# A two-layer hybrid mixer: the last layer's merge and output with tokens on partitions, and work that needs no stream at the border of the layers

## The chip, the cores and the metric

One core of a Trainium2 chip runs the whole kernel. The metric is device time in microseconds from launch to end. The kernel before was timed three times: 1225.44, 1225.52 and 1230.26, a median of 1225.52. Besides these there is one profiled execution, from which every duration below is read.

The engines are TensorE (PE; its weight loads are shown apart as PEld), VectorE (DVE), ScalarE (ACT), GpSimd (POOL) and SyncE (SP, which here issues the DMAs).

## What is computed

Two layers of a mixer with D = 1024 over 256 latent tokens and 256 context tokens. In each layer four branches read one normalised input h. Every branch is gated, projected to D, and summed under a sigmoid gate of its own; one output product, an RMS norm and a gate add the sum to the stream. The second layer computes no context output.

```python
def merge_branches(ys, h, w, w_branch_l, w_out_l):
    merged = None
    for r in range(N_BRANCH):
        term = jax.nn.sigmoid(in_proj(h, w, 'gate_%d' % r)) * (ys[r] @ w_branch_l[r])
        merged = term if merged is None else merged + term
    return merged @ w_out_l
...
    for l in range(DEPTH):
        sh_x, sc_x, gt_x = jnp.split(silu_c @ w_ada[l] + b_ada[l], 3, axis=-1)
        hx = rmsnorm(x, g_pre[l]) * (1.0 + sc_x[:, None]) + sh_x[:, None]
        ya, ya_c = na_branch(hx, hc, w, na_rpb[l], cos, sin, rows, with_ctx)
        yb = fourier_branch(hx, w, fnet_w[l])
        yc = gmlp_branch(hx, w, gmlp_norm_g[l], gmlp_ws[l], gmlp_bs[l])
        yd, yd_c = hgrn2_branch(hx, hc, w, lower_bounds[l], hgrn_norm_g[l], with_ctx)
        out_x = merge_branches((ya, yb, yc, yd), hx, w, w_branch[l], w_out[l])
        ...
        x = x + gt_x[:, None] * rmsnorm(out_x, g_post[l])
    return x
```

All is float32. The recurrence (hgrn2) is a chain of chunks, which the kernel works out in seven levels for each stream.

## The kernel before

**Layout.** Nearly everything lies with channels on partitions and tokens in the free dimension: h is kept as `hhi` and `hlo`, a high part and a remainder, [128, 8, 512], where columns 0 to 255 are the latent tokens (stream 0) and 256 to 511 the context (stream 1). Layer 0 works on both, layer 1 on the latent tokens; names carry the layer first (`w1a_g0`, `h10` is layer 1, stream 0).

**Products.** A weight tile is 128x1024 float32, 512 KB, loaded on SP's queue and split into a high part by ACT and a remainder by DVE. A product is then three matmuls for each block of 128 channels: high times low, low times high, high times high. `proj` does eight such blocks (24 matmuls) for 128 output channels, with the weight as the stationary operand and the tokens as the moving one: 512 columns in layer 0, 256 in layer 1. Products whose output lies with tokens on partitions (a_v, c_v, d_i) are already turned round: the tokens are stationary and 512 weight columns move.

**Merge and output.** `merge(r, ...)` does a branch r in eight groups of 128 output channels: a gate product g (24 matmuls), its sigmoid, the branch product g..b (12 matmuls), then on DVE the multiplication and the addition to `mg`. The last branch splits the sum into `mh` and `ml`. `finish(s)` takes these through the output product o (8 times 24 matmuls); for each block ACT squares o (`osq`), DVE sums the squares (`oacc`) and writes `O`, o times the gate G. `residual` then sums over partitions with small matmuls (`r10oss`; the name is layer, stream, o), takes the inverse root in small DVE steps (`r10ov` to `r10o_y`), spreads it over the partitions by a matmul (`r10oR`), multiplies, adds to the residual stream `xr` and sends it out. For layer 0 it goes on to the norm, scale and shift of layer 1 (`r00x..`, `r01x..`), which write hhi and hlo (`scale_shift`).

**Order.** The program is written as a list of tasks, generators that yield between blocks of matmuls. Each engine runs its instructions in the order in which they are issued. Chains that shouldn't hold PE up (recurrence, residual, attention) are spawned as generators of their own; the class `Order` resumes one as soon as a model of the engines' clocks says that its inputs are ready, between two blocks of the main list, or at a `wait(name)`. It also issues the weight loads and splits, at most three raw tiles and four split ones in flight. PSUM has a ring of three tiles for large products (`ps_big`), one of three for small ones (`ps_sm`) and one of one.

**Start.** `start()` goes through the eight channel blocks j. The adaLN row products `ada` run two steps ahead; in step j a small transposition `adaT` of that row gives scale and shift (`scA`, `shB`, on DVE), `scale_shift` makes x into hhi (ACT) and hlo (DVE) of block j, and `more(j)` lets the first five projections (`firstw0d_f_fwd`, ..) take up the blocks below j, so that these products grow block by block.

Of the kernel before, what the change touches and what calls it, by code (L numbers as in the profile page):

```python
# [19 lines left out]
D = 1024  # L20
# [297 lines left out]
def block(ctx: ExitStack, tc: tile.TileContext, a: dict, out: bass.AP):  # L318
# [32 lines left out]
    def big(shape, name, dt=F32):  # L351
        return slot.tile(shape, dt, name=name, tag="slot")
# [148 lines left out]

    def residual(s, x, O, acc, name, last):

        over4 = lambda R: V(R, 0, [[0, 4], [1, 256]])
        R = yield from rms_rows(sum_rows(acc, name + "o"), 2, name + "o")
        if last:
            Rs = t2k.tile([128, 256], F32, name="Rs", tag="t1k", bufs=3)
            act.activation(Rs, R, AF.Copy)
            for eng, js in ((gps, range(6, 8)), (dve, range(0, 2)), (dve, range(2, 4)), (dve, range(4, 6))):
                n, q, c = len(js), js[0] // 4, slice(js[0] % 4, js[0] % 4 + len(js))  # L510
                eng.tensor_tensor(out=O[q][:, c, :], in0=O[q][:, c, :], in1=V(Rs if eng is gps else R, 0, [[0, n], [1, 256]]),
                                  op=ALU.mult)
                eng.tensor_tensor(out=x[q][:, c, :], in0=x[q][:, c, :], in1=O[q][:, c, :], op=ALU.add)
                sync.dma_start(out[:, js[0]:js[0] + n, :], x[q][:, c, :])
            return
        for q in range(2):
            dve.tensor_tensor(out=O[q], in0=O[q], in1=over4(R), op=ALU.mult)
            dve.tensor_tensor(out=x[q], in0=x[q], in1=O[q], op=ALU.add)
            act.activation(O[q], x[q], AF.Square)
        dve.tensor_tensor(out=O[0], in0=O[0], in1=O[1], op=ALU.add)  # L520
        for n in (2, 1):
            dve.tensor_tensor(out=O[0][:, 0:n, :], in0=O[0][:, 0:n, :], in1=O[0][:, n:2 * n, :], op=ALU.add)
        yield
        R = yield from rms_rows(sum_rows(O[0][:, 0, :], name + "x"), 2, name + "x")
        for q in range(2):
            y = O[q]
            dve.tensor_tensor(out=y, in0=x[q], in1=over4(R), op=ALU.mult)
            for jj in range(4):
                scale_shift(4 * q + jj, s, y[:, jj, :])
# [23 lines left out]
    def start(first, rest):  # L553
# [42 lines left out]
        for j in range(NK):  # L596
            dve.tensor_tensor(out=xT[j // 2][:, j % 2, :], in0=xT[j // 2][:, j % 2, :], in1=R, op=ALU.mult)
            if 1 <= j <= len(first):
                key, _ = first[j - 1]
                w = od.take(key)  # L600
                ps = places[j - 1]("first" + key)
                gens.append([proj(ps, w, slice(0, 512)), 0, ps])
            if j + AHEAD < NK:
                rows.append(ada(j + AHEAD))
            more(j)
            tps = ps_hg(f"adaT{j}")[:, 0, :]
            for i in range(2):
                mm(tps[:, 2 * i:2 * i + 2], lhsT=rows[j][:, i * 128:i * 128 + 128], rhs=sel, start=True, stop=True)
            dve.tensor_scalar(out=shB[:, :, j], in0=tps[:, 0:2], scalar1=bada[:, 0, j:j + 1], scalar2=None, op0=ALU.add)
            dve.tensor_scalar(out=scA[:, :, j], in0=tps[:, 2:4], scalar1=bada1[:, j:j + 1], scalar2=gpre[:, 0, j:j + 1],  # L610
                              op0=ALU.add, op1=ALU.mult)
            for s in range(2):
                scale_shift(j, s, xT[j // 2][:, j % 2, s * 256:s * 256 + 256])
        rest()
        for (gen, _, ps), (_, done) in zip(gens, first):
# [33 lines left out]
    def layer(l, stream, first):  # L649
# [450 lines left out]
        def silu_held(ps, name):  # L1100
# [3 lines left out]
            return sh  # L1104

        def fourier_tasks():
            y2 = new_y('B')
            ab = []

            def f():  # L1110
                ab.append(big([128, 4, 256], f"f{l}AB"))
                od.spawn(f"B{l}.w", fourier_weights(ab[0]))
                yield
            task(f)
            for q in range(2):
# [84 lines left out]

        mg2 = bigs(8, nQ, f"mg{l}")
        mh, ml = bigs(8, nQ, f"mh{l}", F32R, "FK" if L0 else None), bigs(8, nQ, f"ml{l}", F32R)
        G = sml.tile([128, 2, 8], F32, name=f"gg{l}", tag="gg", bufs=2)

        def merge(r, y2, need, fill=(), turn=1, ms=range(8), cols=allc):
# [3 lines left out]
            for m in ms:  # L1209
# [35 lines left out]
                task(f)  # L1245

        def finish(s):

            keys = [unit(f"wo{l}{s}{j}", a["wout"][l, j]) for j in range(8)]

            def f():
                x = stream[s]
                if L0:
                    x = [big([128, 4, 256], f"xr{s}{q}") for q in range(2)]
                    for q in range(2):
                        sync.dma_start(x[q], a["xT"][:, 4 * q:4 * q + 4, s, :])
                O = [big([128, 4, 256], f"O{l}{s}{q}") for q in range(2)]
# [19 lines left out]
                stream[s] = x  # L1277
                od.spawn(f"h{l + 1}.{s}", residual(s, x, O, acc, f"r{l}{s}", not L0))
            task(f)
# [18 lines left out]
        if L0:  # L1298
# [15 lines left out]
            merge(2, yC, None, fill[16:])  # L1314
        else:
            wait("h1.0")
            yA, attend = attention_gates()
            yB = fourier_tasks()
# [3 lines left out]
            then(lambda: I_open.__setitem__(0, False))  # L1322
            merge(1, yB, (f"B{l}",), turn=0)
            attend()
            wait(f"D{l}.0")
            hgrn_proj(1)
            merge(0, yA, (f"A{l}",))
            yC = gmlp_tasks()
            merge(2, yC, None)
# [5 lines left out]
        then(gates)  # L1335
        if L0:
            merge(3, yD, None, turn=3, ms=range(LATEM))
            merge(3, yD, None, turn=3, ms=range(LATEM, 8), cols=slice(0, 256))
            finish(0)
            merge(3, yD, None, turn=3, ms=range(LATEM, 8), cols=slice(256, 512))  # L1340
            finish(1)
        else:
            merge(3, yD, None, turn=3)
            finish(0)
        return tasks
# [74 lines left out]
def _layout(p):  # L1420
# [17 lines left out]
    cols = np.concatenate([np.arange(512) + 512 * NAMES.index(n) for n in TGROUPS])  # L1438
    o["wtk"] = c(win[:, :, cols].reshape(2, 4, 2, 128, 3, 512).transpose(0, 4, 1, 3, 2, 5))
    o["wbr"] = c(g["w_branch"].reshape(2, 4, 4, 128, 4, 2, 128).transpose(0, 1, 4, 3, 5, 2, 6).reshape(2, 4, 4, 128, 8, 128))  # L1440
    o["wout"] = c(g["w_out"].reshape(2, 8, 128, 8, 128).transpose(0, 3, 2, 1, 4))
# [32 lines left out]
```

## Time and profile before

| | |
|---|---|
| median of three runs | 1225.52 us |
| the profiled execution's own time | 1227.05 us |
| its span | 1225.2 us |
| granted TensorE clock, mean | 0.994 |
| DMA traffic | 163.35 MB, mean 133 GB/s |
| weight tiles of the gates (wg) | 66 loads of 512 KB, 3.4 us each to landing |
| largest groups of the chain that ended last | PE g 22%, PE a_v 4%, PE ak 4%, PE o 3% |

The page gives busy time, share and number of instructions of each engine for the whole span; PE's busy time is of matmuls that overlap, so a row of one matmul shows a duration longer than the distance to the next. A row of the timeline is start, duration, engine, line, operation, output<-inputs, tile shapes and count; in square brackets stands how long the engine had been idle before it, and whose result ended the wait. A row of the chain of waits is start, duration, engine, tile and count. The windows give the same busy times for a stretch of the span. Every operation goes through a helper, so the lines are nearly all L131 (matmul), L141 (transpose) and L157 (the other engines), and the tile names tell them apart.

### The profile page before, as it was taken

The numbers are of one execution on the slowest core, as the hardware profiler recorded it, in microseconds if no ns is written. First come the engines' busy times: TensorE is split into PE (matmuls) and PEld (weight loads), VectorE is DVE, ScalarE is ACT, GpSimd is POOL, SyncE is SP. The second block draws the span as 40 slices with busy tenths as digits, with TensorE's granted clock in tenths as the row PEclk, the third lists the DMA queues.
The fourth block names the chain that finished last, engine by engine and source line by source line (L and its number), as shares of the span: only waits on it lengthen the run. The fifth ranks groups of instructions, "written<-read, shape, count | busy, mean of one in ns | idle before, by whom it ended". The sixth has DMA issues, their size and how long they took to land.

```text
span 1225.2 us, 21723 instructions
## 1 busy us (share of the span) xinstructions
PE 1182.2 (96%) x9028; PEld 1006.8 (82%) x9028; DVE 782.7 (64%) x1412; ACT 507.9 (41%) x789; POOL 4.8 (0%) x10
## 2 busy tenths in 40 slices
PE   4999999999999999999999999999999999999995
PEld 2677887777788888888888899988898779989995
DVE  5458346765854469746863578968553877866565
ACT  4553324464333222233223346554343555444451
POOL 0000000000000000000000000000000000000000
PEclk9999999999999999999999999999999999999998
DMA  9621222222214245633673374533253324455551
GB/s 364 218 67 65 87 70 90 81 72 86 71 55 144 92 133 193 195 119 115 196 237 105 101 246 153 170 106 122 87 155 121 106 85 129 148 166 170 173 189 52
DMA packets 52034, 163.35 MB, mean 133 GB/s; under 512 B 6752, under 2 KB 13536, under 8 KB 51936
## 3 DMA queue, kind: packets, MB, share of 16 engines
q1 hardware_dynamic: 51936, 161.96, 40.2%
q8 instruction: 71, 1.16, 0.4%
q14 instruction: 27, 0.22, 0.1%
HBM read 160.89 MB, written 1.05 MB: 132 GB/s over the span
## 4 chain that ended last, share of the span: by engine, by line
PE 89%; DVE 6%; ACT 2%; issue 1%; DMA 1%; SPq 0%; ACTq 0%; DVEq 0%
PE g L131 22%; PE a_v L131 4%; PE ak L131 4%; PE o L131 3%; PE zd_f_fwd L131 3%; PE zd_f_bwd L131 3%; PE bx L131 3%; PE aq L131 3%; PE c_v L131 3%; PE d_i L131 3%; PE bg L131 2%; PE dg L131 2%; PE ag L131 2%; PE q L131 2%; PE ao L131 2%
## 5 line engine op out<-in xcount | busy, mean ns | idle before, releaser
L157 ACT ACTIVATE mh<-mg 128x256 fp32r<-128x256 f32 (+1 forms) x18 | 8.7, 488 | 22.3 <-DVE mg L157 22.3
L157 DVE TENSOR_SCALAR F<-F,om,lb 128x512 f32<-128x512 f32 x8 | 4.4, 548 | 20.6 <-ACT F L157 20.6
L157 ACT ACTIVATE osq<-o 128x256 f32<-128x256 f32 x21 | 8.0, 382 | 21.9 <-PE o L131 21.7
L157 DVE TENSOR_TENSOR oacc<-oacc,osq 128x256 f32<-128x256 f32 x21 | 8.9, 423 | 12.6 <-ACT osq L157 12.6
L157 ACT ACTIVATE xT<-xT,shB,scA 128x256 f32<-128x256 f32 x16 | 8.7, 594 | 16.5 <-DVE scA L157 16.5
L157 ACT ACTIVATE QK<-ak 128x512 f32<-128x512 f32 x8 | 4.8, 598 | 25.5 <-PE ak L131 25.5
L157 DVE TENSOR_SCALAR F<-F 128x512 f32<-128x512 f32 x16 | 6.8, 425 | 12.0 <-ACT F L157 12.0
L157 ACT ACT_TABLE_LOAD x11 | 14.1, 1283 | 0.9 <-PEq L1464 0.7
L157 DVE TENSOR_TENSOR ml<-mg,mh 128x256 fp32r<-128x256 f32 (+1 forms) x18 | 9.2, 513 | 7.3 <-ACT mh L157 7.3
L157 DVE TENSOR_SCALAR O<-o,gg 128x256 f32<-128x256 f32 x24 | 11.5, 479 | 2.3 <-ACT oacc L157 2.3
L157 ACT ACTIVATE yhA<-ya 128x512 fp32r<-128x512 f32 (+1 forms) x8 | 4.2, 526 | 20.0 <-DVE ya L157 20.0
L131 PE MATMUL x0ss<-ones,xacc 128*32 128x1 f32 x32 | 0.6, 194 | 12.2 <-DVE xacc L157 12.2
L157 DVE TENSOR_TENSOR Q<-Q,F 128x1024 f32<-128x1024 f32 (+1 forms) x12 | 11.4, 953 | 0.8 <-PE h01d L131 0.4
L157 DVE TENSOR_TENSOR ya<-ao,sa 128x512 f32<-128x512 f32 (+1 forms) x8 | 4.5, 556 | 11.4 <-PE ao L131 11.4
L131 PE MATMUL ada<-wa,cs 128*32 128x256 f32 x128 | 11.6, 465 | 0.0
L131 PEld LDWEIGHTS h00l<-Q,h00ki 64*64 64x64 f32 x448 | 7.6, 135 | 4.5 <-issue 4.1
L157 DVE TENSOR_SCALAR shB<-adaT,c_bada 128x2 f32<-128x2 f32 x8 | 1.8, 222 | 14.6 <-PE adaT L131 14.6
L157 ACT ACTIVATE h01ki<-K 128x1024 f32<-128x1024 f32 x7 | 8.1, 1153 | 7.2 <-DVE K L157 7.2
L157 ACT ACTIVATE h00ki<-K 128x1024 f32<-128x1024 f32 x7 | 8.1, 1162 | 5.9 <-DVE K L157 5.9
L131 PEld LDWEIGHTS x0ss<-ones,xacc 128*32 128x32 f32 x32 | 0.6, 153 | 12.2 <-issue 12.2
L131 PE MATMUL h00l<-Q,h00ki 64*64 64x64 f32 x448 | 8.6, 226 | 1.9 <-DVE Q L157 1.9
L157 ACT ACTIVATE O<-O,shB,scA 128x256 f32<-128x256 f32 x16 | 8.7, 594 | 3.5 <-DVE O L157 3.5
(3335 smaller groups left out, 4599.2 us busy)
## 6 DMA issues: line engine op xcount, KB each, us to landing
wg<-in_win SPq DMA_DIRECT2D x66, 512.0 KB, 3.4
bg<-in_wbr SPq DMA_DIRECT2D x33, 512.0 KB, 3.4
v<-in_wadaT SPq DMA_DIRECT2D x32, 512.0 KB, 3.5
wo<-in_wout SPq DMA_DIRECT2D x24, 512.0 KB, 3.8
wa<-in_wada SPq DMA_DIRECT2D x16, 512.0 KB, 6.8
biast<-in_bias SPq DMA_DIRECT2D x32, 128.0 KB, 2.4
xT<-in_xT SPq DMA_DIRECT2D x4, 512.0 KB, 5.1
w0d_f_fwd<-in_win SPq DMA_DIRECT2D x4, 512.0 KB, 4.7
```

What stands on the lines that cost most here:

```text
L131: self.nc.tensor.matmul(out, lhsT=lhsT, rhs=rhs, **kw)
L157: f(*a, **k)
```

## The change

It has three parts.

**Merge and output of layer 1.** `merge_tokens` takes the place of `merge`, and `finish_tokens` that of `finish`. The tokens are the stationary operand now (128 of them, `tt` 0 and 1) and 512 weight columns move (u 0 and 1); the weights come in new layouts `in_wgt`, `in_wbt` and `in_wot`, again in tiles of 512 KB, each with two blocks of 128 channels by 512 columns. The sum lies in `mT`, tokens on partitions; `turned(u)` transposes it on PE and splits it into mh and ml, spawned as M.0 and M.1 after each half of the last branch. The output product also has tokens on partitions. There the squares are summed by ACT's accumulation (`oss`), `Gr` is the gate spread over the partitions, and the inverse root is one number for each partition, used by one fused multiply and add into `xt`, the residual stream with tokens on partitions. The result is written as (2, 128, 1024).

**The border of the layers.** `fourier_begin` (the tables f10ab, f11ab of the Fourier branch), `gates` and `gate_rows` (Gr) are issued ahead of layer 1's wait for h1.0, and `residual_rows` (xt) behind it.

**The start.** In step j the first projections' turn (`od.take`, `more(j)`) comes behind adaT and scale_shift of that step; before it stood ahead of them.

```diff
-    def residual(s, x, O, acc, name, last):
+    def residual(s, x, O, acc, name):
...
-        if last:
-            Rs = t2k.tile([128, 256], F32, name="Rs", tag="t1k", bufs=3)
-            act.activation(Rs, R, AF.Copy)
...
         for j in range(NK):
             dve.tensor_tensor(out=xT[j // 2][:, j % 2, :], in0=xT[j // 2][:, j % 2, :], in1=R, op=ALU.mult)
-            if 1 <= j <= len(first):
...
-            more(j)
             tps = ps_hg(f"adaT{j}")[:, 0, :]
...
             for s in range(2):
                 scale_shift(j, s, xT[j // 2][:, j % 2, s * 256:s * 256 + 256])
+            if 1 <= j <= len(first):
...
+            more(j)
...
+        def token_product(pss, key, q, last, stat, name):
+
+            hi, lo = od.take(key)
+            for tt in range(2):
+                if q == 0:
+                    pss.append(ps_big(f"{name}{tt}"))
+                c = slice(tt * 128, tt * 128 + 128)
+                for k in range(2 * q, 2 * q + 2):
+                    s = slice(k % 2 * 512, k % 2 * 512 + 512)
+                    mm(pss[tt], lhsT=stat[1](k)[:, c], rhs=hi[:, s], start=k == 0, stop=False)
+                    mm(pss[tt], lhsT=stat[0](k)[:, c], rhs=lo[:, s], start=False, stop=False)
+                    mm(pss[tt], lhsT=stat[0](k)[:, c], rhs=hi[:, s], start=False, stop=k == 2 * last + 1)
...
+        def turned(u):
+
+            for j in (4 * u, 4 * u + 2):
+                ps = ps_sm(f"mt{j}")
+                for k in range(2):
+                    for tt in range(2):
+                        transpose(ps[:, k * 256 + tt * 128:k * 256 + tt * 128 + 128],
+                                  mT(tt)[:, (j + k) * 128:(j + k) * 128 + 128], eye)
+                split(V(mh(j), 0, [[1, 512]]), V(ml(j), 0, [[1, 512]]), ps)
+            yield
+
+        def across(ps_of, src_of, dst, rhs):
+
+            for u in range(2):
+                ps = ps_sm(ps_of + str(u))
+                for j in range(4):
+                    if rhs is None:
+                        transpose(ps[:, j * 128:j * 128 + 128], src_of(4 * u + j), eye)
+                    else:
+                        mm(ps[:, j * 128:j * 128 + 128], lhsT=src_of(4 * u + j), rhs=rhs, start=True, stop=True)
+                act.activation(dst[:, u * 512:u * 512 + 512], ps, AF.Copy)
...
+                yield ("M.0", "Gr")
+                for u in range(2):
+                    pss = []
+                    for q in range(4):
+                        if u == 0 and q == 2:
+                            yield ("M.1",)
+                        for tt in token_product(pss, keys[u][q], q, 3, (mh, ml), f"o{u}"):
+                            if tt is not None:
+                                c = slice(u * 512, u * 512 + 512)
+                                sq = t2k.tile([128, 512], F32, name=f"osq{u}{tt}", tag="t2k")
+                                act.activation(sq, pss[tt], AF.Square, accum_out=ss[:, tt, u:u + 1])
+                                dve.tensor_tensor(out=O(tt)[:, c], in0=pss[tt], in1=Gr(0)[:, c], op=ALU.mult)
+                            yield
+                for tt in range(2):
...
+                    r = rsqrt(v, [128, 1], f"or{tt}")
+                    for u in range(2):
+                        c = slice(u * 512, u * 512 + 512)
+                        dve.scalar_tensor_tensor(out=xt(tt)[:, c], in0=O(tt)[:, c], scalar=r, in1=xt(tt)[:, c],
+                                                 op0=ALU.mult, op1=ALU.add)
+                        sync.dma_start(out[tt, :, c], xt(tt)[:, c])
...
+            then(fourier_begin)
+            then(gates)
+            then(lambda: od.spawn("Gr", gate_rows()))
             wait("h1.0")
+            then(lambda: od.spawn("xt", residual_rows(stream[0])))
```

Where the instructions stand. On PE in the prologue before the change, around the transposition of the fifth block, `adaT4` (`ada` are the row products, the `first..` rows belong to the first projections):

```order
L131 MATMUL firstw0d_f_bwd1_378<-hlo_89,w0d_f_bwd1h_244 128x512
L131 MATMUL firstw0d_f_bwd1_378<-hhi_88,w0d_f_bwd1l_245 128x512
L131 MATMUL firstw0d_f_bwd1_378<-hhi_88,w0d_f_bwd1h_244 128x512
L131 MATMUL adaT4_419<-c_sel_106,adarows4_348 128x2 x2
L131 MATMUL ada6_434<-wa60_339,cs_133 32x256 x4
L131 MATMUL firstw0d_q0_433<-hlo_89,w0d_q0hl_303 128x512
```

and with the change:

```order
L131 MATMUL ada4_333<-wa41_271,cs_133 32x256 x4
L131 MATMUL firstw0d_f_fwd1_365<-hlo_89,w0d_f_fwd1h_201 128x512
L131 MATMUL firstw0d_f_fwd1_365<-hhi_88,w0d_f_fwd1l_202 128x512
L131 MATMUL firstw0d_f_fwd1_365<-hhi_88,w0d_f_fwd1h_201 128x512
L131 MATMUL adaT4_403<-c_sel_106,adarows4_352 128x2 x2
L131 MATMUL firstw0d_f_fwd0_286<-hlo_89,w0d_f_fwd0h_161 128x512
L131 MATMUL firstw0d_f_fwd0_286<-hhi_88,w0d_f_fwd0l_162 128x512
L131 MATMUL firstw0d_f_fwd0_286<-hhi_88,w0d_f_fwd0h_161 128x512
L131 MATMUL firstw0d_f_bwd0_322<-hlo_89,w0d_f_bwd0h_165 128x512
```

adaT4 stood behind ada5 and all matmuls of the new projection first..bwd1 (the rows ahead of it); now it stands ahead of them, right behind ada4 and the matmuls of the step before. So it goes on to the end of the start: between adaT6 and adaT7, the last, 28 rows of first projections (two rounds of fifteen matmuls, those of blocks 5 and 6) stood before the change and 14 stand now, so that the round of block 6 lies behind adaT7, between it and the round of block 7, which needs it.

On PE at the border of the layers before the change (`ag11` is a gate product of layer 1's attention, `r01oss` the sum of squares of the context stream):

```order
L131 MATMUL ag11_6793<-hlo_89,w1a_g1h_6663 128x256
L131 MATMUL ag11_6793<-hhi_88,w1a_g1l_6664 128x256
L131 MATMUL r01oss_6742<-ones_111,oacc01_6395 32x1 x8
L131 MATMUL ag11_6793<-hhi_88,w1a_g1h_6663 128x256
L131 MATMUL ag11_6793<-hlo_89,w1a_g1h_6663 128x256
```

and with the change:

```order
L131 MATMUL ag11_6861<-hhi_88,w1a_g1l_6664 128x256
L131 MATMUL r01oss_6745<-ones_111,oacc01_6395 32x1 x8
L131 MATMUL f10ab_6770<-wf_132,c_dftc_130 128x128 x4
L131 MATMUL f11ab_6776<-wf_132,c_dftc_130 128x128 x4
L131 MATMUL Gr0_6784<-eye8_109,gg1_122 128x128 x4
L131 MATMUL Gr1_6790<-eye8_109,gg1_122 128x128 x4
L141 MATMUL xt00_6799<-c_eye_100,xr00_5965 128x128 x4
L141 MATMUL xt01_6805<-c_eye_100,xr01_5966 128x128 x4
L131 MATMUL r01oR_6811<-eye8_109,r01o_y_6759 128x128 x2
L141 MATMUL xt10_6830<-c_eye_100,xr00_5965 128x128 x4
L141 MATMUL xt11_6836<-c_eye_100,xr01_5966 128x128 x4
L131 MATMUL ag11_6861<-hhi_88,w1a_g1h_6663 128x256
```

The Fourier tables, Gr and xt now stand in the midst of ag11, with r01oR among them. Before, f10ab and f11ab stood in a product of the Fourier branch (bx100) and r01oR in ag13. The 24 matmuls of ag10 stand ahead of all these rows in both.

On DVE at the end, before the change, the sum of squares and the beginning of the inverse root:

```order
L157 TENSOR_SCALAR O101_11529<-o106_11730,gg1_122 128x256
L157 TENSOR_TENSOR oacc10_11530<-oacc10_11530,osq1_11784 128x256
L157 TENSOR_SCALAR O101_11529<-o107_11759,gg1_122 128x256
L157 TENSOR_SCALAR r10ov_11797<-r10oss_11788 128x2
L157 TENSOR_SCALAR r10o_i_11799<-r10ov_11797 128x2
L157 TENSOR_SCALAR r10o_i_11799<-r10o_i_11799 128x2
```

and the last rows behind it:

```order
L157 SCALAR_TENSOR_TENSOR r10o_y_11802<-r10o_t_11803,r10o_y_11802 128x2
L157 TENSOR_TENSOR O100_11528<-O100_11528,r10oR_11813 128x512 x2
L157 TENSOR_TENSOR xr00_5965<-xr00_5965,O100_11528 128x512 x2
L157 TENSOR_TENSOR O101_11529<-O101_11529,r10oR_11813 128x512
L157 TENSOR_TENSOR xr01_5966<-xr01_5966,O101_11529 128x512
```

With the change the last rows are these (`or1` is the inverse root of the second half of the tokens, `Ot` the gated output):

```order
L157 TENSOR_TENSOR or0_t_11060<-or0_t_11060,or0_y_11059 128x1
L157 SCALAR_TENSOR_TENSOR or1_y_11080<-or1_t_11081,or1_i_11077 128x1
L157 SCALAR_TENSOR_TENSOR or0_y_11059<-or0_t_11060,or0_y_11059 128x1
L157 SCALAR_TENSOR_TENSOR or1_t_11081<-ov1_11074,or1_y_11080 128x1
L157 SCALAR_TENSOR_TENSOR xt_0_6798<-Ot_0_10980,or0_y_11059,xt_0_6798 128x512 x2
L157 TENSOR_TENSOR or1_t_11081<-or1_t_11081,or1_y_11080 128x1
L157 SCALAR_TENSOR_TENSOR or1_y_11080<-or1_t_11081,or1_y_11080 128x1
L157 SCALAR_TENSOR_TENSOR or1_t_11081<-ov1_11074,or1_y_11080 128x1
L157 TENSOR_TENSOR or1_t_11081<-or1_t_11081,or1_y_11080 128x1
L157 SCALAR_TENSOR_TENSOR or1_y_11080<-or1_t_11081,or1_y_11080 128x1
L157 SCALAR_TENSOR_TENSOR xt_1_6829<-Ot_1_10991,or1_y_11080,xt_1_6829 128x512 x2
```

The sum of squares, the multiplication by r10oR and the addition are gone from DVE's end; in their place stand the small steps of two halves, drawn into one another, and fused operations of 512 columns.

More of the change, by code (lines that the diff above doesn't have):

```diff
@@ L613, in start @@
                 scale_shift(j, s, xT[j // 2][:, j % 2, s * 256:s * 256 + 256])
+            if 1 <= j <= len(first):
+                key, _ = first[j - 1]
+                w = od.take(key)
+                ps = places[j - 1]("first" + key)
+                gens.append([proj(ps, w, slice(0, 512)), 0, ps])
+            more(j)
         rest()
@@ new lines, in merge_tokens, with f @@
+        def merge_tokens(r, y2, need, turn=1):
+            for u in range(2):
+                n_ = f"g{l}{r}{u}"
+                kg = [unit(f"w{n_}{q}", a["wgt"][r, u, q]) for q in range(4)]
+                kb = [unit(f"b{n_}{q}", a["wbt"][r, u, q]) for q in range(2)]
+                def f(u=u, n_=n_, kg=kg, kb=kb):
+                    gp, sg, bp = [], [], []
+                    h = (lambda k: hhi[:, k, :], lambda k: hlo[:, k, :])
+                    for q, key in enumerate(kg):
+                        for tt in token_product(gp, key, q, 3, h, n_):
+                            if tt is not None:
+                                sg.append(sig(gp[tt], n_))
+                            yield
+                    yield need
+                    for q, key in enumerate(kb):
+                        for tt in token_product(bp, key, q, 1, y2, n_ + "b"):
+                            if tt is not None:
+                                mg = mT(tt)[:, u * 512:u * 512 + 512]
+                                if turn == 0:
+                                    dve.tensor_tensor(out=mg, in0=bp[tt], in1=sg[tt], op=ALU.mult)
+                                else:
+                                    dve.tensor_tensor(out=sg[tt], in0=bp[tt], in1=sg[tt], op=ALU.mult)
+                                    dve.tensor_tensor(out=mg, in0=mg, in1=sg[tt], op=ALU.add)
+                            yield
+                    if turn == 3:
+                        od.spawn(f"M.{u}", turned(u))
+                task(f)
@@ L1251, in f @@
             def f():
[L1252 to L1256, printed above, removed]
+                x = [big([128, 4, 256], f"xr{s}{q}") for q in range(2)]
+                for q in range(2):
+                    sync.dma_start(x[q], a["xT"][:, 4 * q:4 * q + 4, s, :])
                 O = [big([128, 4, 256], f"O{l}{s}{q}") for q in range(2)]
@@ L1277, in f @@
                 stream[s] = x
-                od.spawn(f"h{l + 1}.{s}", residual(s, x, O, acc, f"r{l}{s}", not L0))
+                od.spawn(f"h{l + 1}.{s}", residual(s, x, O, acc, f"r{l}{s}"))
             task(f)
@@ L1322, in layer @@
             then(lambda: I_open.__setitem__(0, False))
-            merge(1, yB, (f"B{l}",), turn=0)
+            merge_tokens(1, yB, (f"B{l}",), turn=0)
             attend()
@@ L1326, in layer @@
             hgrn_proj(1)
-            merge(0, yA, (f"A{l}",))
+            merge_tokens(0, yA, (f"A{l}",))
             yC = gmlp_tasks()
-            merge(2, yC, None)
+            merge_tokens(2, yC, None)
         wait(f"D{l}")
@@ L1334, in layer @@
             then(lambda: set_mod(1, mod1[:, 0:8, :], mod1[:, 8:16, :]))
-        then(gates)
         if L0:
+            then(gates)
             merge(3, yD, None, turn=3, ms=range(LATEM))
@@ L1342, in layer @@
         else:
-            merge(3, yD, None, turn=3)
-            finish(0)
+            merge_tokens(3, yD, None, turn=3)
+            finish_tokens()
         return tasks
@@ L1468 @@
         args[name] = nc.dram_tensor("in_" + name, v.shape, mybir.dt.from_np(v.dtype), kind="ExternalInput").ap()
-    out = nc.dram_tensor("out", (128, 8, 256), F32, kind="ExternalOutput").ap()
+    out = nc.dram_tensor("out", (2, 128, 1024), F32, kind="ExternalOutput").ap()
     with tile.TileContext(nc) as tc:
```

57 lines of the change are left out of this document (38 added, 19 removed).

## The prediction

> **What bounds the kernel now.** I read the page first, then the windows by stage, then the chain of waits stage by stage, then the timeline at the three places that the change touches. The page's span, busy line and chain by engine:
>
> ```profile
> span 1225.2 us, 21723 instructions
> PE 1182.2 (96%) x9028; PEld 1006.8 (82%) x9028; DVE 782.7 (64%) x1412; ACT 507.9 (41%) x789; POOL 4.8 (0%) x10
> PE 89%; DVE 6%; ACT 2%; issue 1%; DMA 1%; SPq 0%; ACTq 0%; DVEq 0%
> ```
>
> TensorE is busy 96% of the span and is 89% of the chain that ends last, so what counts is PE's own time and the few places where PE idles. The windows say where those are; the columns are the stretch, its length, then busy time and count of PE, PEld, DVE, ACT and POOL, the granted clock, the DMA share and GB/s:
>
> ```profile
> 21.40:70.70 49.30, 42.87 (x244) 29.84 (x245) 23.62 (x58) 28.06 (x54) 0.00 (x0) 0.97 0.63 227
> 780.00:1118.70 338.70, 334.83 (x2945) 296.39 (x2944) 231.92 (x461) 160.59 (x262) 0.00 (x0) 1.00 0.39 126
> 1118.70:1211.20 92.50, 92.44 (x769) 92.04 (x767) 55.96 (x85) 40.84 (x62) 0.00 (x0) 1.00 0.49 154
> 1211.20:1226.00 14.80, 1.50 (x20) 1.18 (x20) 7.62 (x20) 0.75 (x2) 2.88 (x2) 0.57 0.20 71
> ```
>
> In the rest of the prologue PE idles 6.4 of 49.3 us. In the last layer it is full, and in its last merge and output (third row) the weight loads are full too: 92.04 us for 767 loads, 0.120 us each. The tail (fourth row) has no products: 14.8 us in which the end waits for a chain of small work.
>
> **Products with tokens on partitions.** In columns start, duration, what, four pieces of the chain give the price of a product in both shapes:
>
> ```profile
> 918.17 21.79 PE a_v L131 x96
> ...
> 1118.74 2.88 PE g L131 x24
> 1121.62 1.44 PE g1200b L131 x12
> ...
> 1187.86 23.30 PE o L131 x192
> ```
>
> A gate product has 24 matmuls in 2.88 us, a branch product 12 in 1.44, the output 192 in 23.30 (0.121): 0.120 us for 256 columns. a_v already runs with tokens stationary and 512 weight columns: 21.79/96 = 0.227 us. Four merges of eight groups with 36 matmuls are 1152; with the output's 192 that is 1344. The new form has half as many, 672, of 512 columns. A pair of old ones costs 0.240 and one new one 0.227, so 672 × 0.0133 = **-9.0 us** (merges 7.7, output 1.3). Where small matmuls of the recurrence cut into a product, a little of it may go: bounds -9.0 to -8.0. The weight tiles stay 512 KB, and a tile now lasts 12 × 0.227 = 2.72 us rather than 2.88, with DVE busy 56 of 92.5 us there (third window), so loads and splits stay hidden. Sigmoids and multiplies become half as many at twice the width.
>
> [...]
>
> **Turning the merged rows back.** The output product needs channels on partitions, so the sums are transposed: 16 transposes of 128x128.
>
> ```profile
> 1066.86 0.66 PE h11kt L141 x6
> ```
>
> 0.66/6 = 0.11 us, hence **+1.8 us**. The copies and subtractions behind them lie beside products: the first half turns while the second half's gate product runs, and the second half is asked for only after half of the output's first column block (12 + 12 matmuls, 5.4 us). Bounds +1.8 to +4, if the second half is late by one such pair of copies.
>
> **The border of the layers.** Gate rows, the transposed residual and the Fourier tables are now issued there.
>
> ```profile
> 757.46 0.69 PE r00xR L131 x4
> ...
> 767.32 0.36 PE L131 MATMUL ag<-hlo,w1a_g0h 128*128 128x256 f32 x1 [2.00 <-DVE O L157]
> ...
> L157 ACT ACTIVATE QK<-ak 128x512 f32<-128x512 f32 x8 | 4.8, 598 | 25.5 <-PE ak L131 25.5
> ```
>
> Gr is eight f32 matmuls of the kind of r00xR: 8 × 0.17 = 1.4. xt is 16 transposes: 1.8. The tables (f10ab, f11ab), r01oss and r01oR are only moved. PE idles 2.00 us before the first ag, and work without a stream could fill it; but in the new order the 24 matmuls of ag10 still stand ahead of all this work, and ag10 is what waits. I therefore count the filling at nothing. The new PSUM tiles share a ring of three, and each must be copied out by ACT in 0.60 us, while PE makes one in 0.44 (four transposes at 0.11). Over six tiles that is 0.9 us of waiting. Sum **+4.1 us**; bounds +1.1 (the 2.0 filled and no ring wait) to +6 (ACT held up ahead of the copies). Smaller waits: the recurrence's normalisation now has 17 matmuls of 512 columns (3.9 us) between h10ms and h10r as cover.
>
> ```profile
> 890.82 0.17 DVE L157 TENSOR_SCALAR h10v<-h10ms 128x8 f32<-128x8 f32 x1 [0.82 <-PE h10ms L131]
> ...
> 895.62 0.43 DVE L157 TENSOR_SCALAR h10rb<-h_y 128x512 f32<-128x512 f32 x1
> ```
>
> DVE takes 895.62 + 0.43 - 890.82 = 5.2 us for it there, with two weight splits of 1.23 put between; with one fewer it is some 4.2. I add **+0.5 us**, bounds 0 to 2.
>
> **The prologue.** The step adaT → shB, scA → xT → hhi → hlo is a chain over three engines, and the old code queued it behind the previous step's products.
>
> ```profile
> 53.80 0.36 PE L131 MATMUL adaT<-c_sel,adarows 128*128 128x2 f32 x2
> 55.35 0.50 PE L131 MATMUL firstw0d_f_fwd<-hlo,w0d_f_fwd0h 128*128 128x512 f32 x1 [1.19 <-DVE hlo L157]
> ...
> 62.36 0.50 PE L131 MATMUL adaT<-c_sel,adarows 128*128 128x2 f32 x4
> 62.90 0.22 DVE L157 TENSOR_SCALAR shB<-adaT,c_bada 128x2 f32<-128x2 f32 x1 [2.21 <-PE adaT L131]
> 63.22 1.22 DVE L157 TENSOR_TENSOR w0a_g0l<-w0a_g,w0a_g0h 128x1024 fp32r<-128x1024 f32 x1
> 63.34 1.09 ACT L157 ACTIVATE xT<-xT,shB,scA 128x256 f32<-128x256 f32 x2 [3.23 <-DVE scA L157]
> 64.77 0.76 DVE L157 TENSOR_TENSOR hlo<-xT,hhi 128x256 fp32r<-128x256 f32 x2 [0.34 <-ACT hhi L157]
> 65.59 0.50 PE L131 MATMUL firstw0d_f_fwd<-hlo,w0d_f_fwd0h 128*128 128x512 f32 x1 [2.73 <-DVE hlo L157]
> ...
> 66.93 0.63 PE L131 MATMUL firstw0d_f_bwd<-hhi,w0d_f_bwd0l 128*128 128x512 f32 x1
> 67.36 0.63 PE L131 MATMUL firstw0d_f_bwd<-hhi,w0d_f_bwd0h 128*128 128x512 f32 x1
> ...
> 70.73 0.39 PE L131 MATMUL q<-hlo,w0d_q1h 128*128 128x512 f32 x1
> ```
>
> The last adaT goes at 62.36 and its hlo lets PE go on at 65.59: 3.2 us, of which 2.73 idle. Now the last adaT stands ahead of the fifteen matmuls of step 6, 15 × 0.227 = 3.4 us of cover. So 2.73 goes, and 1.19 the same way. After the 2.73 the matmuls come every 0.43 us (66.93 to 67.36) rather than 0.23, for some nine of them: 9 × 0.20 = 1.8 us, which goes with the idle time. Together 5.7 us. What may be late next is hlo of step 6, since ACT has both steps' xT and hhi on it and DVE's splits stand between; I keep 0.7 for that: **-5.0 us**, bounds -6.5 (small waits further ahead go too) to -2 (one wait of 2.7 stays in another place). The first products after 70.73 follow at once, on weights that are split long before.
>
> [...]
>
> **The tail.**
>
> ```profile
> 1210.86 0.28 PE L131 MATMUL o<-mh,wo107h 128*128 128x256 f32 x1
> 1211.18 0.39 ACT L157 ACTIVATE osq<-o 128x256 f32<-128x256 f32 x1 [2.49 <-PE o L131]
> ...
> 1212.17 0.31 PE L131 MATMUL r10oss<-ones,oacc 128*32 128x1 f32 x16 [1.03 <-DVE oacc L157]
> 1212.54 0.16 DVE L157 TENSOR_SCALAR r10ov<-r10oss 128x2 f32<-128x2 f32 x1
> ...
> 1214.70 0.16 DVE L157 SCALAR_TENSOR_TENSOR r10o_y<-r10o_t,r10o_y 128x2 f32<-128x2 f32 x1
> ...
> 1215.01 1.20 PE L131 MATMUL r10oR<-eye,r10o_y 128*128 128x128 f32 x4 [2.54 <-DVE r10o_y L157]
> ...
> 1216.66 1.28 DVE L157 TENSOR_TENSOR O<-O,r10oR 128x512 f32<-128x512 f32 x2 [1.79 <-ACT Rs L157]
> ...
> 1217.86 2.35 DVE L157 TENSOR_TENSOR xr<-xr,O 128x512 f32<-128x512 f32 x2
> ...
> 1220.85 0.69 DVE L157 TENSOR_TENSOR xr<-xr,O 128x512 f32<-128x512 f32 x1
> ```
>
> From the start of the last output matmul to the end of the last addition is 1221.54 - 1210.86 = 10.7 us. Afterwards: 0.45 to the square, 0.8 for a square of 512 columns with its sum (0.60 for a copy of that size, and an allowance of 0.2 for the sum), 13 small DVE steps at 0.2 (the twelve from 1212.54 to 1214.86 take 2.3) = 2.6, then four fused multiply-adds of 128x512, two for the other half of the tokens and two of its own, at about 0.69 (the last row) = 2.8. That is 6.7: **-4.0 us**, bounds -4.3 to -3.5 with the steps of the two halves interleaved. The wait for r10oR, the copy Rs and POOL's part are gone; the four last transfers are as large as before, 3.7 us after the last addition.
>
> **Sum.** -9.0 + 1.8 + 4.1 + 0.5 - 5.0 - 4.0 = -11.6. The profiled execution took 1227.05 us (span 1225.2), so 1215.4; it lies 1.5 above the median 1225.52 of three runs (1225.44 to 1230.26), and taken from that the forecast is **1213.9**.
>
> **Rivals.**
> (a) The prologue gains nothing, because ACT or DVE there is as late as before: its window has ACT busy 28 of 49 us and DMA at 0.63, and only three waits carry the gain. Sum -6.6: 1218.9. Against it: fifteen matmuls of cover for a chain of 3.2 us.
> [...]
> (c) The change doesn't hide what it says: the turned second half or the border's ring is late at both bounds (+2.2 and +1.9), and the recurrence at +2: 1219.5.
> (d) Slower: in the last layer the recurrence's seven levels of two scans lose their cover. Each level waits on DVE for the next Q; if the order of the new merge puts two weight splits (2 × 1.22) between, which nothing covers, 14 × 2.4 = 34 us come on top: 1248. It decides from the point where DVE needs more between two levels than PE's fill. Against it: the new order has 12 to 18 matmuls of 512 columns (2.7 to 4.1 us) between two levels of the second scan, 21 to 33 of 256 (2.5 to 4.0) before; and the first scan already runs over blocks of twelve such matmuls with a wait of 0.19:
>
> ```profile
> 865.17 0.69 PE L131 MATMUL h10l<-Q,h10ki 64*64 64x64 f32 x32 [0.19 <-DVE Q L157]
> ```
>
> With a single split uncovered at each level it would be 17 us, 1231, about no change.
>
> **How the numbers follow.** Forecast (1209.5 to 1218) 0.70; (a) 0.11; (b) 0.06; (c) 0.07; (d) 0.06, of which half beyond 1231.6. The range is 1209.5 to 1220: it takes in (a), (c) and the terms' bounds, not all of them at their best or worst at once, and leaves out (b) and (d). Half a per cent (6.1 us) is about what a measurement of this kernel can tell from no change: below 1219.4 is faster, above 1231.6 slower. Faster holds the forecast, (a) and part of (c): 0.83; within 0.5% holds (b), the rest of (c) and half of (d): 0.14; slower 0.03.
>
> **What would show it.** Rights: products of 24 matmuls g in 5.4 us; q's first matmul at about 65.7 rather than 70.73, no wait above 1 us after 55; 6.7 us from the last o to the last xt; PE full through the last 90 us. Wrong: waits of PE named DVE Q or mh in the last layer, a wait at xt or Gr over 1 us, or a pace of g over 0.23.

## The result

| | median | runs |
|---|---|---|
| before | 1225.74 us | 1225.44 to 1230.26 (4) |
| with the change | 1216.59 us | 1215.91 to 1217.26 (4) |
| ratio | 0.9914 | 95% interval 0.9897 to 0.9932 |

The change makes the kernel 9.1 us faster. 1213.9 had been forecast, with 1209.5 to 1220 as the range. The profiled execution of the changed kernel took 1216.82 us, of before 1227.05, so between the two traces there are 10.2 us; the profile of before is one of its longer executions, 1.3 us over the median.

The page of the changed kernel, span, engines and chain as they were shown of before:

```profile
span 1215.0 us, 20355 instructions
PE 1177.9 (97%) x8384; PEld 971.9 (80%) x8384; DVE 776.1 (64%) x1381; ACT 510.1 (42%) x774; POOL 1.9 (0%) x8
PE 88%; DVE 6%; ACT 3%; issue 1%; DMA 1%; SPq 0%; DVEq 0%; ACTq 0%
```

PE has 644 matmuls fewer but only 4.3 us less to do: a wide matmul does the work of two. The other 6 us are idle time of PE that is gone, in the start and the tail. Where they went shows when the same instruction is found in both traces. First the rows of before that the prediction doesn't have (the first product of the recurrence's q in layer 1, and its first level), from the timeline of PE:

```profile
834.68 0.28 PE L131 MATMUL q<-hlo,w1d_q0h 128*128 128x256 f32 x1
850.84 0.89 PE L131 MATMUL h10l<-Q,h10ki 64*64 64x64 f32 x32 [0.20 <-DVE Q L157]
```

and the five marks in the changed kernel:

```profile
66.94 0.39 PE L131 MATMUL q<-hlo,w0d_q1h 128*128 128x512 f32 x1
...
763.31 0.36 PE L131 MATMUL ag<-hlo,w1a_g0h 128*128 128x256 f32 x1 [1.92 <-DVE O L157]
...
834.40 0.28 PE L131 MATMUL q<-hlo,w1d_q0h 128*128 128x256 f32 x1
850.56 0.89 PE L131 MATMUL h10l<-Q,h10ki 64*64 64x64 f32 x32 [0.21 <-DVE Q L157]
...
1203.86 0.39 PE L131 MATMUL o<-wo113h,mh 128*128 128x512 f32 x1
```

| stretch | before | after | difference | forecast |
|---|---|---|---|---|
| launch to q of layer 0 | 70.73 | 66.94 | -3.8 | -5.0 |
| to the first ag (layer 0) | 696.59 | 696.37 | -0.2 | 0 |
| to q of layer 1 (the border) | 67.36 | 71.09 | +3.7 | +4.1 |
| to the first level of the recurrence | 16.16 | 16.16 | 0 | 0 |
| to the last output matmul (products, transposes, small waits) | 360.02 | 353.30 | -6.7 | -9.0 + 1.8 + 0.5 = -6.7 |
| to the end of the span | 14.34 | 11.14 | -3.2 | -4.0 |
| sum | 1225.2 | 1215.0 | -10.2 | -11.6 |

**The products.** In the chain of waits of the changed kernel (start, duration, what) the last merge and the output read:

```profile
1147.92 10.88 PE g L131 x48
1164.24 1.81 PE g L131 x8
1166.05 0.22 PE mt L141 x2
1166.27 0.23 PE g L131
1166.50 0.71 PE mt L141 x6
1167.21 8.88 PE g L131 x39
...
1184.50 18.40 PE o L131 x81
```

48 matmuls of 512 columns take 10.88 us, 0.227 each, as a_v did before. The transposition mt of the first half goes in between gate matmuls at 0.11 to 0.12 us each, and PE waits for none of it.

**The border.** The same view there:

```profile
767.01 0.24 PE r01oss L131 x16
767.24 1.09 PE f10ab L131 x8
768.33 0.89 PE f11ab L131 x8
769.23 1.79 PE Gr L131 x16
771.01 0.87 PE xt L141 x8
771.89 0.63 PE r01oR L131 x4
772.51 0.87 PE xt L141 x8
773.39 6.71 PE ag L131 x56
```

Gr 1.79 and xt 1.74 us are new; r01oss stood here before, the other rows were elsewhere. All are in the chain, one behind the other, with no wait among them: the ring of three PSUM tiles holds nothing up. And the wait ahead of the first ag is still there, 1.92 us where it was 2.00.

**The tail**, from the timeline:

```profile
1203.64 0.69 DVE L157 TENSOR_TENSOR Ot<-o,Gr 128x512 f32<-128x512 f32 x1 [7.34 <-ACT osq L157]
...
1204.34 0.60 ACT L157 ACTIVATE osq<-o 128x512 f32<-128x512 f32 x1 [0.73 <-PE o L131]
...
1205.08 0.68 DVE L157 TENSOR_TENSOR Ot<-o,Gr 128x512 f32<-128x512 f32 x1
...
1207.22 1.41 DVE L157 SCALAR_TENSOR_TENSOR xt<-Ot,or_y,xt 128x512 f32<-128x512 f32 x2
...
1209.52 1.41 DVE L157 SCALAR_TENSOR_TENSOR xt<-Ot,or_y,xt 128x512 f32<-128x512 f32 x2
```

The last operation ends at 1210.93, 7.1 us after the last matmul's start (10.7 before). Behind it there are 4.1 us to the end of the span, 3.7 before. A second trace of the changed kernel (further down) has 4.1 as well, while the six runs below that keep this tail and change something else have 3.0 to 3.3. Why that is so wasn't found; 1 us of the differences below lies there, behind all work that was changed.

### The profile page after: what moved, and what is told of

Read it like the earlier page. It is cut to its first block, busy times and chain, and to the rows that moved or that the text cites. A ratio compares the mean times of both kernels' runs of the same rounds, so it can differ in the third digit from the quotient of the medians.

```text
span 1215.0 us, 20355 instructions
## 1 busy us (share of the span) xinstructions
PE 1177.9 (97%) x8384; PEld 971.9 (80%) x8384; DVE 776.1 (64%) x1381; ACT 510.1 (42%) x774; POOL 1.9 (0%) x8
## 4 chain that ended last, share of the span: by engine, by line
PE 88%; DVE 6%; ACT 3%; issue 1%; DMA 1%; SPq 0%; DVEq 0%; ACTq 0%
PE g L131 21%; PE a_v L131 4%; PE ak L131 4%; PE o L131 3%; PE zd_f_fwd L131 3%; PE zd_f_bwd L131 3%; PE aq L131 3%; PE c_v L131 3%; PE bx L131 3%; PE d_i L131 3%; PE ag L131 2%; PE q L131 2%; PE dg L131 2%; PE bg L131 2%; PE ao L131 2%
## 5 line engine op out<-in xcount | busy, mean ns | idle before, releaser
L157 ACT ACTIVATE osq<-o 128x256 f32<-128x256 f32 (+1 forms) x18 | 7.7, 430 | 19.4 <-PE o L131 19.4
L157 ACT ACTIVATE mh<-mg 128x512 fp32r<-128x512 f32 (+1 forms) x10 | 5.4, 546 | 13.0 <-DVE mg L157 13.0
L157 ACT ACTIVATE z<-bx 128x512 f32<-128x512 f32 (+1 forms) x8 | 3.9, 492 | 15.2 <-PE bx L131 15.2
L157 ACT ACTIVATE adarows<-ada 128x256 f32<-128x256 f32 x8 | 3.1, 382 | 16.9 <-PE ada L131 16.8
L157 DVE COPY_PREDICATED h01Sd<-masks,h01l 128x1024 f32<-128x1024 uint8 x6 | 7.9, 1319 | 3.4 <-PE h01l L131 3.4
```

Of the source, the lines that this page charges most:

```text
L157: f(*a, **k)
```

## The experiments

The traces agree with the sum in most terms. What they leave open: whether a matmul's fixed cost is what the products gain by, whether the start gives its part alone, and whether the border's cost has to be paid.

**The start alone**, in the kernel before:

```diff
-            if 1 <= j <= len(first):
...
-            more(j)
             tps = ps_hg(f"adaT{j}")[:, 0, :]
...
                 scale_shift(j, s, xT[j // 2][:, j % 2, s * 256:s * 256 + 256])
+            if 1 <= j <= len(first):
...
+            more(j)
```

> The kernel before with the start's change alone. Theory: the five parts of the change are independent, and the start gives what the trace of the changed kernel shows there, the first matmul of q at 66.9 rather than 70.7 us: -3.8 us, 1221.9 against 1225.7. Rival: layer 0 gives part of it back, because weights or constants land later than the earlier products want them: -1 to -2 us with a wait of PE behind 70 us, 1224. By the prediction's own sum it would be -5.0 us.

1222.32 us (1222.08 to 1222.79) beside 1226.98 of before on the same chip, ratio 0.9955 (0.9938 to 0.9972): 4.7 us by the medians. In its trace q's first matmul is 3.5 us sooner:

```profile
67.20 0.39 PE L131 MATMUL q<-hlo,w0d_q1h 128*128 128x512 f32 x1
```

PE has no new wait in layer 0. The start stands by itself, and its size is about that of the changed kernel's trace.

**Products in halves**, in the changed kernel (the same for the other two matmuls of the block):

```diff
-                    mm(pss[tt], lhsT=stat[1](k)[:, c], rhs=hi[:, s], start=k == 0, stop=False)
+                    for e in (0, 256):
+                        mm(pss[tt][:, e:e + 256], lhsT=stat[1](k)[:, c], rhs=hi[:, s.start + e:s.start + e + 256], start=k == 0 and e == 0, stop=False)
```

> The changed kernel with each product of 512 weight columns in the merge and the output done as two of 256 (1344 matmuls again, tokens still on partitions). Theory: a matmul has a fixed cost of some 13 ns beside its columns (0.120 us for 256, 0.227 for 512), so the time rises by 672 x 0.0133 = 9.0 us, to 1225.6. [...] If another thing made the merge faster (fewer, wider operations on ACT and DVE), the time would stay near 1216.6.

1223.14 us (1222.14 to 1223.72): 6.5 above the changed kernel's 1216.59, which was measured apart from it; against before, measured beside each of them, the gain shrinks from 9.1 to 3.8, by 5.3. The chain of waits of this kernel, two of the pieces:

```profile
1151.57 11.52 PE g L131 x96
...
1189.92 19.69 PE o L131 x164
```

96 matmuls take 11.52 us where 48 of twice the width took 10.88: 0.64 for each 48, and 14 times that for 672 is 9.0. From the first level of the recurrence to the last output matmul it is 361.54 us against 353.30, +8.2; the rest of the difference to 6.5 lies outside the products, in stretches that this edit doesn't touch. Counted over that whole stretch, start to start and without waits, the matmuls of the merge and the output took 164.6 us before, 156.3 in the changed kernel and 164.8 in halves. So there is a fixed cost of about 13 ns in these matmuls (0.64 us over 48), as the rows of before said. Fewer operations on ACT and DVE, which this kernel has as well, aren't what made the merge faster.

Whether the 13 ns belong to the matmul or to the weight load that each matmul brings isn't shown, since the halves double both. The loads fill the time of the matmuls of 256 columns (92.04 of 92.50 us in the merge and output before), and 9.01 of the 10.88 us in the changed kernel, so loads that no longer fit beneath 256 columns are a rival. Against it: xt's transposes, 128 columns with a load each, come at 0.11 us, faster than the 0.120 of 256 columns.

**The border filled.** Tables and gate rows are issued at once behind the last output product, not spawned:

```diff
-            then(fourier_begin)
-            then(gates)
-            then(lambda: od.spawn("Gr", gate_rows()))
+            def border():
+                ab.append(big([128, 4, 256], f"f{l}AB"))
+                for _ in fourier_weights(ab[0]):
+                    pass
+                gates()
+                for _ in gate_rows():
+                    pass
+            then(border)
             wait("h1.0")
```

> The changed kernel with the Fourier tables and the gate rows issued directly behind the last output product of layer 0, ahead of the context stream's residual, so that on PE they stand between it and the first gate product of layer 1, in the wait of 1.9 us. Theory: that wait is free PE time, and twelve of the small matmuls (1.6 us) go into it; the border's cost falls from 3.7 to about 2.0 us: -1.7 us against the changed kernel, 1214.9. Rival: ACT's four copies and DVE's gate steps stand ahead of hhi and hlo and make the wait longer by as much: no gain, 1216.6.

1213.29 us (1212.32 to 1213.87), ratio to before 0.988 (0.9863 to 0.9897). The timeline of PE:

```profile
760.54 1.05 PE L131 MATMUL f10ab<-wf,c_dftc 128*128 128x128 f32 x8
761.43 1.06 PE L131 MATMUL f11ab<-wf,c_dftc 128*128 128x128 f32 x8
762.33 1.06 PE L131 MATMUL Gr<-eye,gg 128*128 128x128 f32 x8
763.14 0.36 PE L131 MATMUL ag<-hlo,w1a_g0h 128*128 128x256 f32 x1
```

The wait ahead of ag is gone, filled by 2.6 us of work. From the last block's first matmul (o<-ml,wo017h at 757.72) to ag it is 5.4 us, where the changed kernel has 4.9 (758.38 to 763.31), so PE reaches ag only 0.5 us later and has three of the four tiles behind it. The stretch from ag to the q of layer 1 falls from 71.09 to 831.12 - 763.14 = 67.98 us, by 3.1. Together that is -2.6 us, more than the 1.7 expected. The twelve matmuls that went ahead of ag had been counted at 0.13 us each and take 0.22 (2.6 us from 760.54 to 763.14), so they fill the whole wait of 1.92. The other 0.7 is in rows behind ag that take less time, most of it in the Fourier branch's product bx (96 matmuls, start to start 11.8 us rather than 12.4); why they do wasn't followed up.

The difference to the changed kernel was then measured on one chip:

> The changed kernel once more, on the same chip as the other two of this call. Theory: 1216.6 +- 0.7, ratio 0.992.

> The border filled once more (the kernel of e3_border_fill). Theory: 2.5 to 3.3 us below the changed kernel on the same chip; rival: the difference between the calls was the chip's, and both stand within 1 us.

1216.44 us (1215.15 to 1217.13) and 1212.69 (1211.97 to 1213.09), ratios to before 0.9911 (0.9892 to 0.9931) and 0.9879 (0.9857 to 0.9901). The medians differ by 3.8 us, the two profiled spans by 2.1 (1213.4 and 1211.3). The border explains 2.6 of it, and 0.8 lies behind the last operation (3.3 us to the end against 4.1, as above). The filled border beats the changed kernel, by 2 to 4 us.

**The border late.** Gate rows and residual go ahead of the last branch's merge, the tables back into the Fourier branch:

```diff
-            then(fourier_begin)
-            then(gates)
-            then(lambda: od.spawn("Gr", gate_rows()))
             wait("h1.0")
-            then(lambda: od.spawn("xt", residual_rows(stream[0])))
             yA, attend = attention_gates()
+            then(fourier_begin)
...
+            then(gates)
+            then(lambda: od.spawn("Gr", gate_rows()))
+            then(lambda: od.spawn("xt", residual_rows(stream[0])))
             merge_tokens(3, yD, None, turn=3)
```

> The changed kernel with gate rows and transposed residual issued ahead of the last branch's merge, and the Fourier tables back in the Fourier branch. Theory: the 3.1 us of small f32 matmuls are PE time wherever they stand, and only the waits for PSUM at the border (0.6 us) go: -0.6 us against the changed kernel, 1216.0. Rival: they fall into waits that the last layer has anyway, -2 us or more, 1214.5.

1215.71 us (1215.48 to 1216.61), 0.9 below the changed kernel, near the theory and within what separates two measurements of one kernel. From ag to the last output matmul it took 1203.42 - 762.40 = 441.0 us, against 440.6 in the changed kernel: the time is the same wherever the work stands, except in a wait. The 0.6 us of PSUM waits that were to go aren't in the changed kernel's trace either.

**The residual in the attention's waits.** With the border filled, xt is moved to where PE waits 1.0 us for the probabilities, twice:

```diff
                     od.spawn(f"A{l}.{m}", attention(m, (q, qr, k, kr), Vt, sa(m), y2))
+                    if not L0 and m in (0, 2):
+                        od.spawn(f"xt.{m}", residual_rows(stream[0], m // 2))
...
-            then(lambda: od.spawn("xt", residual_rows(stream[0])))
```

> The border filled as in e3_border_fill, and the transposed residual made in layer 1's attention: one half behind the first pair of heads, the other between the transposed probabilities and their product, where PE waited 1.0 us for DVE. Theory: work without a stream costs nothing where PE idles, so of the 2.0 us of transposes about 1.0 vanishes: 1212.3. Rival: the transposes take PSUM of the attention's own ring and put a copy on ACT in its chain, so that the wait grows: 1213.3 or more.

1216.07 us (1215.73 to 1217.23): 3.4 above the filled border on the same chip, the rival. PE's waits in this kernel (waited for, us in total, times, longest):

```profile
PE xt L141 <- DVE a1000mx L157: 1.3, 1, 1.3
PE ao L131 <- DVE a10PT L157: 1.0, 1, 1.0
PE xt L141 <- DVE a12PT L157: 1.0, 1, 1.0
```

The transposes themselves wait now, 1.3 and 1.0 us, for DVE to be through with tiles of the attention, whose PSUM ring they share. The filled border has the 1.0 for a12PT too, there ahead of ao: the second half of xt didn't fill that wait but stands in it, and what was behind it on PE still comes after it. The 1.3 is new. The traces differ by 3.1 us (spans 1214.4 and 1211.3): 1.4 is PE's waits, and 1.6 is rows that take longer start to start, xt (2.2 us for 1.6) and the attention's a120s and a121s (2.9 for 1.9); the cause of these wasn't looked for. Work without a stream is not work without a wait.

**The tail joined**, one inverse root of two columns:

```diff
-                for tt in range(2):
-                    v = sml.tile([128, 1], F32, name=f"ov{tt}", tag="ov")
-                    dve.tensor_tensor(out=v, in0=ss[:, tt, 0:1], in1=ss[:, tt, 1:2], op=ALU.add)
...
-                    r = rsqrt(v, [128, 1], f"or{tt}")
+                v = sml.tile([128, 2], F32, name="ov", tag="ov")
+                dve.tensor_tensor(out=v, in0=ss[:, :, 0], in1=ss[:, :, 1], op=ALU.add)
...
+                r = rsqrt(v, [128, 2], "or")
```

> The changed kernel with one inverse root of two columns for both halves of the tokens in place of two interleaved ones. Theory: the small DVE steps cost their distance of 0.19 us one behind the other, not their number: 13 steps from 1.2 us after the last output matmul, then four fused operations of 0.70, so the last one ends 6.5 us after that matmul's start rather than 7.1, -0.6 us in the trace; too little for the median to settle. Rival: the first half's fused operations and its transfers start later than now, and the transfers set the end: 0 to +0.5 us.

1214.86 us (1214.36 to 1216.07). The median is 1.7 below the changed kernel's, but the trace doesn't put it in the steps that were changed: the last output matmul starts at 1203.03, and DVE reads

```profile
1204.24 0.69 DVE L157 TENSOR_TENSOR Ot<-o,Gr 128x512 f32<-128x512 f32 x1 [0.73 <-ACT osq L157]
1204.85 0.15 DVE L157 TENSOR_TENSOR ov<-oss 128x2 f32<-128x2 f32 x1
...
1207.40 2.74 DVE L157 SCALAR_TENSOR_TENSOR xt<-Ot,or_y,xt 128x512 f32<-128x512 f32 x4
```

so the last operation ends at 1210.14, 7.1 us after that matmul, as in the changed kernel. The thirteen steps do take 2.55 us (1204.85 to 1207.40), 0.196 each. The expectation missed that the product Ot stands ahead of them on DVE, and that it starts only when ACT's square is through: 1.8 us to the first small step, not 1.2. What the joint chain saves (two fused operations no longer ahead of part of the second root) it loses again to its later start. Behind the last operation there are 3.1 us to the end rather than 4.1; that is 1.0 of the 1.7, but runs that leave the tail alone have it as well.

**The row products behind adaT**, in the start:

```diff
-            if j + AHEAD < NK:
-                rows.append(ada(j + AHEAD))
             tps = ps_hg(f"adaT{j}")[:, 0, :]
...
                 scale_shift(j, s, xT[j // 2][:, j % 2, s * 256:s * 256 + 256])
+            if j + AHEAD < NK:
+                rows.append(ada(j + AHEAD))
```

> The changed kernel with the next block's row product (ada) issued behind adaT and scale_shift of the step. Theory: what is left of waits in the prologue (1.4 us for hlo at 32 us, 0.4 at 60) comes from the chain of three engines standing behind work that doesn't need it; adaT goes on PE ahead of eight matmuls of ada, 1 us sooner in each step: -1 to -1.5 us at q's first matmul (66.9 in the changed kernel). Rival: the loads of ada's weights set the pace until 30 us (DMA share 1.0), so the waits only move: 0 us.

1216.90 us (1216.51 to 1217.15). The first matmul of q is at 66.41, half a microsecond sooner, no more than it moves between executions of the same start (66.94 and 65.96 in the two traces of the changed kernel). The time is the rival's: the waits only moved, 2.2 us for hlo remain, 1.8 of them at 30 us. But the rival's reason is not borne out, and the theory isn't tested cleanly. Two windows of this kernel and of the changed one, in this order:

```profile
25.00:30.00 5.00, 2.88 (x20) 1.84 (x16) 2.13 (x8) 3.49 (x7) 0.00 (x0) 0.82 0.36 138
30.00:35.00 5.00, 4.92 (x21) 3.11 (x22) 2.44 (x5) 1.81 (x3) 0.00 (x0) 0.66 0.56 193
...
25.00:30.00 5.00, 5.00 (x32) 2.36 (x28) 2.68 (x7) 0.81 (x2) 0.00 (x0) 1.00 1.00 379
30.00:35.00 5.00, 3.42 (x27) 1.91 (x19) 1.27 (x6) 2.86 (x7) 0.00 (x0) 1.00 0.65 258
```

The DMA share (the last but one) is 0.36 ahead of the wait, so the loads don't set the pace there. And behind the wait of 1.8 us the granted clock is 0.66: a slow stretch like that of before has come up here. Thirteen matmuls on PE (five of the first projections and eight row products) take 3.5 us from 30.08 to 33.61 where the changed kernel does as many in 2.0 from 31.82 to 33.85. So some of what the edit saves may have gone to the clock again, an estimated 1.5 us; that it would gain without the slow stretch isn't shown. (ada runs one step ahead in all these kernels, AHEAD = 1, not two.)

**Border and tail together.**

> The border filled (as in e3_border_fill) and the tail joined (as in e5_tail_joined). Theory: the two are independent, 1213.3 - 0.6 = 1212.7, ratio to the kernel before 0.988 +- 0.002. Rival: no better than the border alone, 1213.3 or more.

1212.92 us (1212.64 to 1213.02), ratio 0.9892 (0.9871 to 0.9913): as the border alone, as the tail gives nothing; the 0.6 between theory and rival is less than two measurements of one kernel differ by.

## Why the prediction was right, and where its sizes were off

**Products and transposes** came out to a tenth as a sum, -6.7 us between the first level of the recurrence and the last output matmul, and the halves show the cause, the fixed 13 ns. The terms were each a little too large, and that they cancel is luck: products -8.3 for -9.0, transposes +1.5 for +1.8, new waits +0.2 for +0.5 (start to start). The chance of 0.06 was put on (b), that the products gain only part of this. No run shows the smaller fixed cost that it takes: the halves rose by 8.2 us in the trace, 12 ns for each of 672. The waits that were feared in the recurrence are there and small: PE waits 0.2 us more for DVE at one level of the second scan (h11l), and none at h10r. Rival (d), levels that lose their cover, does not show.

**The start** gave -3.8 us in this trace, not -5.0. The mechanism is as forecast. PE's waits for hlo fell from 5.7 us in three to 1.8 in two, and the slow stretch is gone. The windows around it (columns as before, the granted clock is the last but two) of before and of the changed kernel:

```profile
65.00:70.00 5.00, 4.41 (x12) 3.50 (x13) 1.46 (x5) 4.20 (x8) 0.00 (x0) 0.66 0.52 157
```

```profile
65.00:70.00 5.00, 5.00 (x24) 4.13 (x23) 2.87 (x6) 5.00 (x10) 0.00 (x0) 1.00 0.56 202
```

The clock stands at 0.66 in one and at 1.00 in the other: the slow stretch went with the idle time, and didn't move elsewhere in layer 0 (1.00 from 66.94 to 763 us). What ties the two isn't shown: behind the 2.00 us ahead of ag the clock of before is 1.00 (767.3 to 770). That it can come up elsewhere shows in the run with the row products behind adaT.

But from 21.4 us to q PE's busy time is the same in both, 42.90 and 42.87 us: the 1.8 of the slow stretch came (1.7, start to start), and PE lost as much again elsewhere in this stretch, in two places. The first lies in the beginning, where matmuls run at the slow pace (0.43 us from one to the next, with a granted clock of 1.00 in the windows) until about 25 us in the trace of before and until about 28 in that of the changed kernel. The eight row products there, of before and of the changed kernel, with the matmul behind them:

```profile
25.99 0.64 PE L131 MATMUL ada<-wa,cs 128*32 128x256 f32 x8
26.56 0.50 PE L131 MATMUL firstw0d_f_fwd<-hlo,w0d_f_fwd0h 128*128 128x512 f32 x1
...
26.77 1.08 PE L131 MATMUL ada<-wa,cs 128*32 128x256 f32 x8
27.79 0.50 PE L131 MATMUL firstw0d_f_fwd<-hlo,w0d_f_fwd0h 128*128 128x512 f32 x1
```

They take 0.57 us in one and 1.02 in the other. Up to here PE's order is the same in both kernels, so this part, about 1 us, is not the new order's doing. It moves between executions: the changed kernel's second trace has q at 65.96, and over the ten traces with this start q stands between 65.96 and 67.20, a gain of 3.5 to 4.8 us against the one trace of before. The second place is the step that failed in the prediction: it counted the 9 × 0.20 us as clear gain and put at nothing that the new order breaks the products up more. Behind a row product or an adaT a matmul of the first projections takes 0.34 us to the next rather than 0.23; between 30 and 62.5 us that is so for 19 of them rather than 13, and with the row products and adaT it costs 0.8 to 1 us. Against that stands the 0.7 that was kept for a late hlo and wasn't needed (a wait of 0.40 at 59.98).

**The border** came out at +3.7 for +4.1, by two errors that partly cancel. Gr was priced at 8 × 0.17 from a row "x4"; those four instructions are two f32 matmuls, as each is two in the profile (Gr: eight matmuls, x16). By f10ab's row in the chain of before (780.61, 0.89 us for four), it would have been 1.8, as measured. The 0.9 for PSUM waits didn't occur. That the new work would not fill the 2.0 us wait was right, and the filled border shows why it matters: spawned work is queued behind r01oss, the context stream's sum of squares, and that comes behind ag.

**The tail**: 10.7 us fell to 7.1 up to the last operation, for 6.7 forecast. The missing 0.4 is Ot ahead of the small steps. The rest of the -3.2 is what comes behind the last operation.

**The whole.** The medians differ by 9.1 us where 11.6 was forecast. Of the 2.5 between, 1.4 are in the terms above; 1.1 is that the sum was read from an execution of before 1.3 us over its median.

**Open.** Runs of one changed kernel differ by 1 to 2 us, those of before by 5, and the parts here are of that size. Why the changed kernel has a microsecond more behind its last operation than the runs beside it isn't known. What the change would give without the start's part wasn't run by itself.

## What to carry to other kernels

Where TensorE is the bound, price a change of tiling by the start-to-start time of a matmul in a row that the kernel already has in the new shape: here half as many matmuls of twice the width (0.227 us for 0.240) saved 13 ns for each pair of old ones. "Needs no stream" helped here only where the work was queued ahead of the instruction that waits and in resources that nobody there held: Gr and xt cost their full 3.5 us behind ag, 2.6 us of such matmuls in front of it made ag only 0.5 us later, and xt within the attention's PSUM ring cost 3 us more than behind ag.

## What was not expected of the hardware

Each of Gr's f32 matmuls of 128x128 is two instructions of 0.11 us in the profile (eight matmuls, x16, in 1.79 us), while each of xt's transposes of the same size is one (eight in 0.87 us). Where ACT squares and DVE multiplies the same PSUM tile, DVE started each of the four times only behind ACT's read (the last osq at 1204.34 for 0.60 and its sum, Ot at 1205.08); two of the rows of Ot in this text name ACT's osq as what ended the wait. Whether the two could read side by side wasn't tried.
